# Retention: a head's output transposes behind all four gate projections, all convolution taps and the norm's root on VectorE

## The chip, the cores and the metric

The program runs on one NeuronCore of a Trainium2 chip. The metric is the device time of one execution in microseconds (us), lower is better. Engines are named as in the profile: PE (TensorE's matmuls), PEld (its weight loads), DVE (VectorE), ACT (ScalarE), POOL (GpSimd), SP (the engine whose queue starts the weight transfers).

## What is computed

Two transformer-like blocks over 512 tokens of width 1024, in float32. The change lies in the second block's mixer, in the stage that computes bidirectional retention (four heads, value width 512 per head) and, beside it, a convolution branch. Cut to these:

```python
q, k, v, rg, cv, ga, gb = split(u @ w_in)
q, k = rope_2d(heads(q, 256)), rope_2d(heads(k, 256)) * scale
o = bidir_retention(q, k, v, log_gf, log_gb, rf, rb)      # per head: decayed scores @ v, 512 x 512

# retention_branch: normalise each token of each head, gate it
mu, var = mean(o, -1), mean(square(o - mu), -1)
of = (o - mu) * rsqrt(var + 1e-6) * gn_w
y_ret = (silu(rg) * of) @ w_ret_out

# conv_branch: 31 taps along the tokens, each channel by itself
a, g = split(cv)
y = depthwise_conv(a * sigmoid(g), conv_w, width=31) + conv_b
y = silu(layernorm(y)) @ w_conv_out
mixed = (sigmoid(ga) * y_ret + sigmoid(gb) * y_conv) @ w_out
```

## The kernel before

Activations lie transposed: 128 channels on the partitions, 512 tokens in the free dimension. Each float32 operand is split in two parts of lower precision, hi (a cast on ACT) and lo (the difference, on DVE or POOL; `split`, line 110 and 111), and each product is three matmuls (`mm3`, lines 144 to 146). A projection of 128 output channels is eight chunks of 1024 input channels, so 24 matmuls into one of three PSUM buffers named `mm`. Its weight comes through a SP transfer, ACT's `whi` and a `wlo`, into one of three pairs of buffers: the weight of the projection three places on can be split only when the present one has ended.

`retention` runs over four heads. For each: `qkv` (four rotary projections `rope` for q and k, then eight value tiles), `scores` (six tiles), two `conv_in` (the convolution's input, two projections each), `av` (the head's output `on`, four query blocks by 18 matmuls), and `finish` (four gate projections and the transposes of `on`). In `av`, ACT copies each block from PSUM, DVE takes mean and variance (`bn_stats`, `bn_aggr`), and the reciprocal root of the four variances is found by three Newton steps on 128x4 tiles; then four DVE instructions (line 1264) normalise `on` in place.

`finish` transposes `on` on PE, four 128x128 transposes for each of the head's four channel groups c (tile `gt`, two PSUM buffers), and DVE multiplies each by weight and gate (`gtd`, line 1278) before POOL's queue writes it to DRAM (`gt_d`).

The convolution's taps are spread over these stages. A tap is one DVE instruction (line 1148, `cz` += weight times a shifted `cy`); taps are queued by `conv_in` and issued by `conv_step` in portions (`TAPS_QK`, `TAPS_V`, `TAPS_IN`, `TAPS_GATE` after a rotary projection, a value tile, a `conv_in`, a gate). Of the 31 taps of each of eight channel groups, 25 run on DVE; six (`CONV_POOL`) are multiplied by ACT (`cpr`) and summed by POOL (`z2`, line 1164), and DVE adds that sum (line 1152). POOL's queue then writes `cz` to DRAM.

The order on each engine is not that of the code alone: a list scheduler with its own time model places instructions; `issue_after` bounds the place of a transpose from below. Behind the last head `mix_out` starts with nine gate projections whose `wlo` are made on POOL (`wpool = (1,)`), then reads the convolution back.

Of the kernel before, what the change touches and what calls it, by code (L numbers as in the profile page):

```python
# [9 lines left out]
F32 = mybir.dt.float32  # L10
F32R = mybir.dt.float32r
I32 = mybir.dt.int32
AF = mybir.ActivationFunctionType
ALU = mybir.AluOpType
# [27 lines left out]

PV_ORDER = ((0, 0), (0, 1), (0, 3), (0, 2), (1, 0), (1, 1), (1, 3), (1, 2))

TAPS_QK, TAPS_V, TAPS_IN, TAPS_GATE = 4, 2, 5, 4
CONV_POOL = 6

GATES_FIRST = 9

# [14 lines left out]
class Kern:  # L64
# [1057 lines left out]
    def retention(self, U):  # L1122
        nc, a, s, tc, tmp = self.nc, self.a, self.small, self.tc, self.tmp
        with ExitStack() as st:
# [1 line left out]
            vp = st.enter_context(tc.tile_pool(reuse_waits=RW, name="convp", bufs=4))  # L1126
            rtab = rp.tile([128, 144], F32, name="rtab")
            nc.gpsimd.dma_start(out=rtab, in_=a["rtab"])
            taps, ptaps = [], []
            cw0 = VEC["cw"][0]  # L1130

            def conv_in(c):
                pa = self.proj(a["w_cv"][c], U)
                pg = self.proj(a["w_cv"][8 + c], U)
                sg = tmp.tile([128, 512], F32, tag="g", name="sg")
                nc.scalar.activation(out=sg, in_=pg, func=AF.Sigmoid)
                y = vp.tile([128, 544], F32, tag="cy", name="cy")
                nc.vector.memset(y[:, 0:15], 0.0)
                nc.vector.memset(y[:, 527:544], 0.0)
                nc.vector.tensor_tensor(out=y[:, 15:527], in0=sg, in1=pa, op=ALU.mult)  # L1140
                z = tmp.tile([128, 512], F32, tag=("lnk", "accd", "accq")[c % 3], name="cz", bufs=1)

                def tap(t):
                    w = self.vec[:, cw0 + c * 31 + t:cw0 + c * 31 + t + 1]
                    if t == 0:
                        nc.vector.tensor_scalar(out=z, in0=y[:, 0:512], scalar1=w, scalar2=self.v("cb", c), op0=ALU.mult, op1=ALU.add)
                    else:
                        nc.vector.scalar_tensor_tensor(out=z, in0=y[:, t:t + 512], scalar=w, in1=z, op0=ALU.mult, op1=ALU.add)  # L1148
                    if t == 30 - CONV_POOL:
                        while ptaps and ptaps[0][0] is ptap:  # L1150
                            ptap(ptaps.pop(0)[1])
                        nc.vector.tensor_tensor(out=z, in0=z, in1=z2, op=ALU.add)
                        nc.gpsimd.dma_start(out=self.z_d[c], in_=z)

                taps.extend((tap, t) for t in range(31 - CONV_POOL))
                prev = None
                z2 = vp.tile([128, 512], F32, tag="z2", name="z2", bufs=2)

                def ptap(t):
                    nonlocal prev  # L1160
                    p = vp.tile([128, 512], F32, tag="cpr", name="cpr", bufs=3)
                    nc.scalar.activation(out=p, in_=y[:, t:t + 512], func=AF.Copy, scale=self.vec[:, cw0 + c * 31 + t:cw0 + c * 31 + t + 1])
                    if prev is not None:
                        nc.gpsimd.tensor_tensor(out=z2, in0=prev, in1=p, op=ALU.add)
                        prev = z2
                    else:
                        prev = p

                ptaps.extend((ptap, t) for t in range(31 - CONV_POOL, 31))

            def conv_step(n):
                for q, m in ((ptaps, max(1, n // 3)), (taps, n)):
                    for _ in range(min(m, len(q))):
                        f, t = q.pop(0)
                        f(t)

            def rope(c, col, tag):
                ps = self.proj(a["w_qk"][c], U)
# [15 lines left out]
            def qkv(hd):  # L1194
                r = {}
                for tag, o in (("q", 0), ("k", 8)):
                    r[tag] = []
                    for col in range(2):
                        r[tag].append(rope(o + 2 * hd + col, col, tag))
                        conv_step(TAPS_QK)  # L1200
                r["td"] = rp.tile([128, 1536], F32, tag="td", name="td")
                nc.gpsimd.dma_start(out=r["td"], in_=self.td_d[hd])
                kc = self.wraw.tile([128, 1024], F32, tag="raw", name="kcr")[:, 0:512]
                nc.gpsimd.dma_start(out=kc, in_=self.kc_d[hd])
                r["kc"] = tuple(rp.tile([128, 512], F32R, tag=f"kc{i}", name=f"kc{i}") for i in "hl")
                self.split(kc, *r["kc"])
                r["v"] = [tuple(rp.tile([128, 512], F32R, tag=f"v{i}{tb}", name=f"v{i}{tb}") for i in "hl") for tb in range(4)]
                for half in range(2):
                    ws = [self.wload(a["w_v"][hd, half, i]) for i in range(2)]
                    for tb in range(4):  # L1210
                        ps = self.ps_mm.tile([128, 512], F32, tag="mm", name="mm")[:, 0:256]
                        self.vproj(ps, ws, U, tb)
                        cs = slice(half * 256, half * 256 + 256)
                        self.split(ps, r["v"][tb][0][:, cs], r["v"][tb][1][:, cs])
                        conv_step(TAPS_V)
                vc = self.wraw.tile([128, 1024], F32, tag="raw", name="vcr")
                nc.gpsimd.dma_start(out=vc, in_=self.vc_d[hd])
                vt = tuple(rp.tile([128, 1024], F32R, tag=f"vc{i}", name=f"vc{i}") for i in "hl")
                self.split(vc, *vt)
                r["vc"] = [tuple(t[:, 512 * i:512 * i + 512] for t in vt) for i in range(2)]  # L1220
                return r
# [22 lines left out]
            def av(hd, r, sc):  # L1244
                os = []
                mv = s.tile([128, 8], F32, tag="gmv", name="gmv")
                for qb in range(4):
                    qs = slice(qb * 128, qb * 128 + 128)
                    ps = self.ps_mm.tile([128, 512], F32, tag="mm", name="mm")
                    vs = r["v"] + r["vc"]  # L1250
                    for b in range(6):
                        self.mm3(ps, tuple(t[:, qs] for t in sc[b]), vs[b], b == 0, b == 5)
                    t = rp.tile([128, 512], F32, tag=("kh0", "kl0", "kh1", "kl1")[qb], name="on")
                    nc.scalar.copy(t, ps)
                    bs = s.tile([128, 6], F32, tag="bns", name="bns")
                    nc.vector.bn_stats(out=bs, in_=t)
                    nc.vector.bn_aggr(out=mv[:, 2 * qb:2 * qb + 2], in_=bs)
                    os.append(t)
                var = s.tile([128, 4], F32, tag="var", name="gvar")
                mv2 = mv.rearrange("p (q t) -> p q t", t=2)  # L1260
                nc.vector.tensor_scalar(out=var, in0=mv2[:, :, 1], scalar1=1e-6, scalar2=None, op0=ALU.add)
                rs = self.rsqrt(var, 4, e=nc.gpsimd)
                for qb in range(4):
                    nc.vector.tensor_scalar(out=os[qb], in0=os[qb], scalar1=mv[:, 2 * qb:2 * qb + 1], scalar2=rs[:, qb:qb + 1],
                                            op0=ALU.subtract, op1=ALU.mult)
                return os

            def finish(hd, os):
                gates, ends = [], []

                def out(c):
                    ch = 4 * hd + c
                    pt = self.ps_t.tile([128, 512], F32, tag="t", name="gt")
                    with tc.issue_after(ends[-1].ins):
                        for qb in range(4):
                            nc.tensor.transpose(out=pt[:, qb * 128:qb * 128 + 128], in_=os[qb][:, c * 128:c * 128 + 128], identity=self.ident)
                    t = tmp.tile([128, 512], F32, tag="t", name="gtd")
                    nc.vector.scalar_tensor_tensor(out=t, in0=pt, scalar=self.v("gnw", ch), in1=gates[c], op0=ALU.mult, op1=ALU.mult)
                    nc.gpsimd.dma_start(out=self.gt_d[ch // 2][:, (ch % 2) * 512:(ch % 2) * 512 + 512], in_=t)

                for c in range(4):
                    ps = self.proj(a["w_rg"][4 * hd + c], U)
                    ends.append(self.last_mm)
                    sg = tmp.tile([128, 512], F32, tag="g", name="sg")
                    nc.scalar.activation(out=sg, in_=ps, func=AF.Silu)
                    gates.append(sg)
                    if c > 0:
                        out(c - 1)
                    conv_step(TAPS_GATE)
                out(3)  # L1290

            for hd in range(4):
                r = qkv(hd)
# [226 lines left out]
```

## Time and profile before

| | |
|---|---|
| median of 3 runs | 3168.19 us (3163.14 to 3169.09) |
| the profiled execution | 3168.4 us, span of the profile 3166.6 us |
| mean granted TensorE clock | 0.982 of full speed |
| busy: PE, DVE, ACT, POOL | 96%, 60%, 38%, 14% of the span |
| retention's four heads | from about 2000 us to 2510 us of the span |

The profile shows one execution. A busy share over the whole span says little about a stage; what an engine waited for, and who released it, is listed for each wait. PE's instructions overlap (a matmul's duration is about 390 ns where a new one starts each 227 ns), so time on PE is read from start to start. The granted clock is that of PE: 1.00 is 2.4 GHz, 0.50 is 1.2 GHz.

### The profile page before, as it was taken

The numbers are of one execution on the slowest core, as the hardware profiler recorded it, in microseconds if no ns is written. First come the engines' busy times: TensorE is split into PE (matmuls) and PEld (weight loads), VectorE is DVE, ScalarE is ACT, GpSimd is POOL, SyncE is SP. The second block draws the span as 40 slices with busy tenths as digits, with TensorE's granted clock in tenths as the row PEclk, the third lists the DMA queues.
The fourth block names the chain that finished last, engine by engine and source line by source line (L and its number), as shares of the span: only waits on it lengthen the run. The fifth ranks groups of instructions, "written<-read, shape, count | busy, mean of one in ns | idle before, by whom it ended". The sixth has DMA issues, their size and how long they took to land.

```text
span 3166.6 us, 41034 instructions
## 1 busy us (share of the span) xinstructions
PE 3046.1 (96%) x15961; PEld 2578.1 (81%) x15961; DVE 1888.0 (60%) x3425; ACT 1192.0 (38%) x1956; POOL 455.0 (14%) x457
## 2 busy tenths in 40 slices
PE   8999999999999999999999999989889899999998
PEld 6678888887778888898888888878778787888887
DVE  4888657575888554473323347687786645553334
ACT  4774322244765222262121127334233243342222
POOL 2320000043310000130000001031121543200000
PEclk9999999999999999999999999999999999999999
DMA  4232445322323554322212126522323324333322
GB/s 131 73 96 75 153 146 186 125 83 79 91 84 101 160 172 130 97 94 85 74 52 76 54 81 220 168 79 95 97 70 104 106 80 146 107 100 94 100 92 62
DMA packets 103650, 334.08 MB, mean 106 GB/s; under 512 B 13164, under 2 KB 16364, under 8 KB 103328
## 3 DMA queue, kind: packets, MB, share of 16 engines
q1 hardware_dynamic: 89232, 289.83, 29.1%
q0 software_dynamic: 13136, 40.59, 4.1%
q8 instruction: 125, 2.05, 0.3%
q10 hardware_dynamic: 1088, 1.05, 0.1%
q14 instruction: 69, 0.57, 0.1%
HBM read 312.51 MB, written 14.71 MB: 103 GB/s over the span
## 4 chain that ended last, share of the span: by engine, by line
PE 58%; DVE 9%; issue 3%; ACT 2%; POOL 1%; DMA 1%; POOLq 0%; DVEq 0%; ACTq 0%
PE mm L145 17%; PE mm L144 17%; PE mm L146 17%; DVE cz L1148 4%; PE gc L144 1%; PE gc L146 1%; PE gc L145 1%; DVE wlo L111 1%; PE dc L146 1%; PE dc L145 1%; PE dc L144 1%; ACT whi L110 0%; PE rs L144 0%; PE rs L145 0%; PE rs L146 0%
## 5 line engine op out<-in xcount | busy, mean ns | idle before, releaser
L110 ACT CAST whi<-raw 128x1024 fp32r<-128x1024 f32 (+3 forms) x524 | 506.6, 968 | 1422.6 <-PE mm L145 1187.0
L145 PE MATMUL mm<-ul,whi 128*128 128x512 f32 (+2 forms) x2288 | 867.0, 380 | 2.1 <-POOL ul L271 1.6
L144 PE MATMUL mm<-uh,whi 128*128 128x512 f32 (+2 forms) x2288 | 866.7, 381 | 0.7 <-ACT cl L645 0.3
L146 PE MATMUL mm<-uh,wlo 128*128 128x512 f32 (+2 forms) x2288 | 864.7, 379 | 1.0 <-DVE wlo L111 0.6
L111 DVE TENSOR_TENSOR wlo<-raw,whi 128x1024 fp32r<-128x1024 f32 (+3 forms) x437 | 505.5, 1158 | 362.9 <-ACT whi L110 355.6
L145 PEld LDWEIGHTS mm<-ul,whi 128*128 128x128 f32 (+1 forms) x2288 | 433.2, 189 | 82.8 <-POOL ul L271 3.2
L146 PEld LDWEIGHTS mm<-uh,wlo 128*128 128x128 f32 (+1 forms) x2288 | 432.5, 189 | 83.2 <-POOL wlo L111 0.9
L144 PEld LDWEIGHTS mm<-uh,whi 128*128 128x128 f32 (+1 forms) x2288 | 432.3, 190 | 81.2 <-ACT uh L267 1.0
L144 PE MATMUL mm<-hh,whi 128*128 128x512 f32 (+1 forms) x789 | 293.6, 372 | 1.4 <-DVE acc L986 0.7
L145 PE MATMUL mm<-hl,whi 128*128 128x512 f32 (+1 forms) x789 | 293.0, 371 | 0.0
L146 PE MATMUL mm<-hh,wlo 128*128 128x512 f32 (+1 forms) x789 | 292.1, 371 | 0.3 <-DVE wlo L111 0.3
L528 DVE TENSOR_TENSOR g<-g,mm 128x512 f32<-128x512 f32 (+1 forms) x96 | 61.7, 643 | 276.9 <-PE mm L146 273.5
L111 POOL TENSOR_TENSOR wlo<-raw,whi 128x1024 fp32r<-128x1024 f32 (+2 forms) x87 | 184.0, 2117 | 236.0 <-ACT whi L110 231.4
L1148 DVE SCALAR_TENSOR_TENSOR cz<-cy,vec,cz 128x512 f32<-128x512 f32 x192 | 176.8, 942 | 2.5
L144 PEld LDWEIGHTS mm<-hh,whi 128*128 128x128 f32 x789 | 151.1, 191 | 27.0 <-issue 1.1
L146 PEld LDWEIGHTS mm<-hh,wlo 128*128 128x128 f32 x789 | 150.7, 191 | 26.6 <-DVE wlo L111 0.7
L145 PEld LDWEIGHTS mm<-hl,whi 128*128 128x128 f32 x789 | 150.9, 191 | 24.8 <-issue 0.2
L986 DVE SCALAR_TENSOR_TENSOR acc<-mm,g,acc 128x512 f32<-128x512 f32 (+1 forms) x61 | 43.1, 707 | 146.8 <-PE mm L146 146.8
L203 POOL TENSOR_TENSOR accd<-acc,acc 128x512 f32<-128x512 f32 x2 | 6.5, 3240 | 650.2 <-DVE acc L483 650.2
L146 PE MATMUL gc<-uch,wlo 128*128 128x256 f32 x352 | 99.4, 282 | 0.2 <-DVE wlo L111 0.2
L144 PE MATMUL gc<-uch,whi 128*128 128x256 f32 x352 | 99.1, 282 | 0.0
L145 PE MATMUL gc<-ucl,whi 128*128 128x256 f32 x352 | 99.0, 281 | 0.0
(407 smaller groups left out, 5230.7 us busy)
## 6 DMA issues: line engine op xcount, KB each, us to landing
mr<-w_mod SPq DMA_DIRECT2D x72, 512.0 KB, 3.9
raw<-w_f1i SPq DMA_DIRECT2D x54, 512.0 KB, 3.5
raw<-w_gate SPq DMA_DIRECT2D x44, 512.0 KB, 3.6
raw<-w_up SPq DMA_DIRECT2D x44, 512.0 KB, 3.5
raw<-w_f2i SPq DMA_DIRECT2D x44, 512.0 KB, 3.5
raw<-w_in SPq DMA_DIRECT2D x36, 512.0 KB, 3.8
raw<-w_v SPq DMA_DIRECT2D x32, 512.0 KB, 4.1
raw<-w_qk SPq DMA_DIRECT2D x24, 512.0 KB, 3.8
```

Of the source, the lines that this page charges most:

```text
L110: nc.scalar.copy(hi, src)
L111: (nc.gpsimd if pool else nc.vector).tensor_tensor(out=lo, in0=src, in1=hi.bitcast(F32), op=ALU.subtract)
L144: mm(out=ps, lhsT=w[0], rhs=x[0], start=first, stop=False)
L145: mm(out=ps, lhsT=w[0], rhs=x[1], start=False, stop=False)
L146: self.last_mm = mm(out=ps, lhsT=w[1], rhs=x[0], start=False, stop=last)
L203: e.tensor_tensor(out=st["accd"][:, sl], in0=(st["D0"] if m == 1 else st["accd"])[:, sl], in1=D[:, sl], op=ALU.add)
L528: gm = nc.vector.tensor_tensor(out=g, in0=g, in1=pu, op=ALU.mult)
L986: self.nc.vector.scalar_tensor_tensor(out=h, in0=ps, scalar=g[:, m:m + 1], in1=h, op0=ALU.mult, op1=ALU.add)
L1148: nc.vector.scalar_tensor_tensor(out=z, in0=y[:, t:t + 512], scalar=w, in1=z, op0=ALU.mult, op1=ALU.add)
```

## The change

Four things, all within `retention`. The transposes of a head's output are no longer placed after the second, third and fourth gate projection: all four gate projections come first, then two groups of transposes, and the other two after the next head's first two rotary projections (for the last head, all four at once). For this the four gates stay in the buffers `sh0` to `sh3` of the scores. All 31 taps of a channel group are DVE instructions; the multiplications on ACT and the sums on POOL are gone, and `TAPS_GATE` is 5. The Newton steps of the norm's root run on DVE rather than POOL.

```diff
-TAPS_QK, TAPS_V, TAPS_IN, TAPS_GATE = 4, 2, 5, 4
-CONV_POOL = 6
+TAPS_QK, TAPS_V, TAPS_IN, TAPS_GATE = 4, 2, 5, 5
...
-                    if t == 30 - CONV_POOL:
-                        while ptaps and ptaps[0][0] is ptap:
-                            ptap(ptaps.pop(0)[1])
-                        nc.vector.tensor_tensor(out=z, in0=z, in1=z2, op=ALU.add)
+                    if t == 30:
                         nc.gpsimd.dma_start(out=self.z_d[c], in_=z)
 
-                taps.extend((tap, t) for t in range(31 - CONV_POOL))
-                prev = None
-                z2 = vp.tile([128, 512], F32, tag="z2", name="z2", bufs=2)
-
-                def ptap(t):
-                    nonlocal prev
-                    p = vp.tile([128, 512], F32, tag="cpr", name="cpr", bufs=3)
-                    nc.scalar.activation(out=p, in_=y[:, t:t + 512], func=AF.Copy, scale=self.vec[:, cw0 + c * 31 + t:cw0 + c * 31 + t + 1])
-                    if prev is not None:
-                        nc.gpsimd.tensor_tensor(out=z2, in0=prev, in1=p, op=ALU.add)
-                        prev = z2
-                    else:
-                        prev = p
-
-                ptaps.extend((ptap, t) for t in range(31 - CONV_POOL, 31))
+                taps.extend((tap, t) for t in range(31))
 
             def conv_step(n):
-                for q, m in ((ptaps, max(1, n // 3)), (taps, n)):
-                    for _ in range(min(m, len(q))):
-                        f, t = q.pop(0)
-                        f(t)
+                for _ in range(min(n, len(taps))):
+                    f, t = taps.pop(0)
+                    f(t)
...
                         r[tag].append(rope(o + 2 * hd + col, col, tag))
+                        flush(1)
                         conv_step(TAPS_QK)
...
-                rs = self.rsqrt(var, 4, e=nc.gpsimd)
+                rs = self.rsqrt(var, 4)
...
+            late = []
+
             def finish(hd, os):
                 gates, ends = [], []
 
-                def out(c):
+                def out(c, after):
...
-                    with tc.issue_after(ends[-1].ins):
+                    with tc.issue_after(after.ins):
...
                 for c in range(4):
                     ps = self.proj(a["w_rg"][4 * hd + c], U)
-                    ends.append(self.last_mm)
-                    sg = tmp.tile([128, 512], F32, tag="g", name="sg")
+
+                    sg = rp.tile([128, 512], F32, tag=f"sh{c}", name="sg")
                     nc.scalar.activation(out=sg, in_=ps, func=AF.Silu)
                     gates.append(sg)
-                    if c > 0:
-                        out(c - 1)
                     conv_step(TAPS_GATE)
-                out(3)
+
+                late.extend(lambda after, c=c: out(c, after) for c in range(4))
+                flush(2 if hd < 3 else 4)
+
+            def flush(n):
+                for _ in range(min(n, len(late))):
+                    late.pop(0)(self.last_mm)
```

What the scheduler makes of it, at three places.

On DVE in the second head, from the last variance to the normalised output (`gvar` is the variance, `rsi` to `rsy` the root, `on` the output, `cz` a tap), before:

```order
L1257 BN_AGGR gmv<-bns 128x2
L1148 SCALAR_TENSOR_TENSOR cz<-cy,vec,cz 128x512
L1261 TENSOR_SCALAR gvar<-gmv 128x4
L1148 SCALAR_TENSOR_TENSOR cz<-cy,vec,cz 128x512
L158 TENSOR_SCALAR rsi<-gvar 128x4
L1148 SCALAR_TENSOR_TENSOR cz<-cy,vec,cz 128x512
L160 TENSOR_SCALAR rsj<-rsi 128x4
L1148 SCALAR_TENSOR_TENSOR cz<-cy,vec,cz 128x512 x3
L1264 TENSOR_SCALAR on<-on,gmv,rsy 128x512 x4
```

and the last rows of the same place in the changed kernel:

```order
L1147 SCALAR_TENSOR_TENSOR cz<-cy,vec,cz 128x512
L169 SCALAR_TENSOR_TENSOR rsy<-rst,rsy 128x4
L1147 SCALAR_TENSOR_TENSOR cz<-cy,vec,cz 128x512
L165 TENSOR_TENSOR rst<-rsy 128x4
L1147 SCALAR_TENSOR_TENSOR cz<-cy,vec,cz 128x512
L166 TENSOR_TENSOR rst<-rst,rsx 128x4
L1147 SCALAR_TENSOR_TENSOR cz<-cy,vec,cz 128x512
L169 SCALAR_TENSOR_TENSOR rsy<-rst,rsy 128x4
L1147 SCALAR_TENSOR_TENSOR cz<-cy,vec,cz 128x512
L1246 TENSOR_SCALAR on<-on,gmv,rsy 128x512 x4
L1147 SCALAR_TENSOR_TENSOR cz<-cy,vec,cz 128x512
```

Before, only the root's first two rows stand here, the rest on POOL, and no row of taps is between the third of three taps and `on`; now all of the root stands here, nearly each of its rows followed by one tap (11 taps and one `wlo` stand between `gvar` and `on`, and two more taps ahead of `gvar`).

On PE behind the last head (`gt` are the transposes, the rows after them the first of `mix_out`'s gate projections), before:

```order
L146 MATMUL mm<-uh_17097,wlo 128x512
L1276 MATMUL gt<-ident,on 128x128 x8
L144 MATMUL mm<-uh_17083,whi 128x512
L145 MATMUL mm<-ul_17084,whi 128x512
L146 MATMUL mm<-uh_17083,wlo 128x512
```

and in the changed kernel:

```order
L145 MATMUL mm<-uh_17097,wlo 128x512
L1260 MATMUL gt<-ident,on 128x128 x8
L143 MATMUL mm<-uh_17083,whi 128x512
L144 MATMUL mm<-ul_17084,whi 128x512
L145 MATMUL mm<-uh_17083,wlo 128x512
L1260 MATMUL gt<-ident,on 128x128 x4
L143 MATMUL mm<-uh_17085,whi 128x512
L1260 MATMUL gt<-ident,on 128x128 x4
L144 MATMUL mm<-ul_17086,whi 128x512
L145 MATMUL mm<-uh_17085,wlo 128x512
```

Before, two groups of four stand one and two projections earlier, and eight transposes come last; now all sixteen stand here, the third and fourth group three and four matmuls behind the first two.

On DVE at the same place in the changed kernel:

```order
L166 TENSOR_TENSOR rst<-rst,rsx 128x4
L1147 SCALAR_TENSOR_TENSOR cz<-cy,vec,cz 128x512
L169 SCALAR_TENSOR_TENSOR rsy<-rst,rsy 128x4
L1147 SCALAR_TENSOR_TENSOR cz<-cy,vec,cz 128x512
L1246 TENSOR_SCALAR on<-on,gmv,rsy 128x512 x4
L1147 SCALAR_TENSOR_TENSOR cz<-cy,vec,cz 128x512 x12
L1262 SCALAR_TENSOR_TENSOR gtd<-gt,vec,sg 128x512 x2
L1147 SCALAR_TENSOR_TENSOR cz<-cy,vec,cz 128x512 x4
L1262 SCALAR_TENSOR_TENSOR gtd<-gt,vec,sg 128x512 x2
L1147 SCALAR_TENSOR_TENSOR cz<-cy,vec,cz 128x512 x4
L190 TENSOR_TENSOR z_22348<-z_22348,lnk 128x512
```

There are twelve taps between the normalised output and the first `gtd`, which frees the PSUM buffer of the third group of transposes. On POOL at the same place (`wlo` are the splits of `mix_out`'s weights), before:

```order
L173 TENSOR_TENSOR rsy<-rst,rsy 128x4
L1153 DMA z_d<-cz 128x512
L111 TENSOR_TENSOR wlo<-raw,whi 128x1024
L1279 DMA gt_d<-gtd 128x512
L111 TENSOR_TENSOR wlo<-raw,whi 128x1024
L1279 DMA gt_d<-gtd 128x512
L1153 DMA z_d<-cz 128x512
L111 TENSOR_TENSOR wlo<-raw,whi 128x1024
```

and in the changed kernel:

```order
L1149 DMA z_d<-cz 128x512
L110 TENSOR_TENSOR wlo<-raw,whi 128x1024 x2
L1149 DMA z_d<-cz 128x512
L110 TENSOR_TENSOR wlo<-raw,whi 128x1024
L1263 DMA gt_d<-gtd 128x512 x4
L1310 DMA z_22348<-z_d 128x512
L1310 DMA z_22357<-z_d 128x512
L110 TENSOR_TENSOR wlo<-raw,whi 128x1024
```

Before, a split came after each write of `gtd`; now three splits stand ahead of the first `gt_d`.

## Rows read from the trace of the kernel before

**Rows 1.** The page, busy time by engine: microseconds, share, instructions.

```profile
PE 3046.1 (96%) x15961; PEld 2578.1 (81%) x15961; DVE 1888.0 (60%) x3425; ACT 1192.0 (38%) x1956; POOL 455.0 (14%) x457
```

**Rows 2.** Waits of TensorE in 2060 to 2516: in total, times, longest.

```profile
PE gt L1276 <- DVE on L1264: 33.2, 4, 8.3
PE gt L1276 <- DVE gtd L1278: 1.4, 1, 1.4
```

**Rows 3.** Busy time, granted clock, DMA share and rate over one head's period.

```profile
2090.87:2217.54 126.67, 118.37 (x606) 100.51 (x605) 98.86 (x136) 43.08 (x60) 26.05 (x33) 0.96 0.28 92
```

**Rows 4.** TensorE in time order around head 0's transposes: start, us, instruction, idle before.

```profile
2101.53 0.39 PE L146 MATMUL mm<-uh,wlo 128*128 128x512 f32 x1
2110.22 1.84 PE L1276 MATMUL gt<-ident,on 128*128 128x128 f32 x4 [8.30 <-DVE on L1264]
2111.72 0.77 PE L144 MATMUL mm<-uh,whi 128*128 128x512 f32 x1
2112.29 0.63 PE L145 MATMUL mm<-ul,whi 128*128 128x512 f32 x1
...
2116.12 0.40 PE L145 MATMUL mm<-ul,whi 128*128 128x512 f32 x1
...
2119.32 0.60 PE L1276 MATMUL gt<-ident,on 128*128 128x128 f32 x4
2119.68 0.47 PE L144 MATMUL mm<-uh,whi 128*128 128x512 f32 x1
2119.99 0.39 PE L145 MATMUL mm<-ul,whi 128*128 128x512 f32 x1
```

**Rows 5.** Busy time and granted clock within and after that gap.

```profile
2101.90:2110.20 8.30, 0.02 (x1) 0.00 (x0) 5.59 (x14) 1.38 (x2) 4.34 (x13) 0.74 0.00 0
2110.30:2115.20 4.90, 4.90 (x12) 3.38 (x13) 4.87 (x10) 0.00 (x0) 0.62 (x1) 0.50 0.26 81
```

**Rows 6.** GpSimd in time order: first and last of the root's 13 instructions.

```profile
2103.56 0.68 POOL L162 TENSOR_SCALAR rsx<-gvar 128x4 f32<-128x4 f32 x1 [11.31 <-DVE gvar L1261]
...
2109.38 0.20 POOL L173 TENSOR_TENSOR rsy<-rst,rsy 128x4 f32<-128x4 f32 x1
```

**Rows 7.** VectorE in time order through the same root.

```profile
2101.32 0.69 DVE L1256 BATCH_NORM_STATS2 bns<-on 128x6 f32<-128x512 f32 x1
...
2103.30 0.17 DVE L1261 TENSOR_SCALAR gvar<-gmv 128x4 f32<-128x4 f32 x1
2103.37 0.75 DVE L1148 SCALAR_TENSOR_TENSOR cz<-cy,vec,cz 128x512 f32<-128x512 f32 x1
...
2109.62 1.92 DVE L1264 TENSOR_SCALAR on<-on,gmv,rsy 128x512 f32<-128x512 f32 x4 [2.71 <-POOL rsy L173]
```

**Rows 8.** VectorE instructions grouped by line, 2066 to 2512.

```profile
L1148 DVE SCALAR_TENSOR_TENSOR cz<-cy,vec,cz 128x512 f32<-128x512 f32 x192 | 176.8, 942 | 2.5
```

**Rows 9.** The chain that ended last, behind the last head: start, us, what.

```profile
2498.80 0.76 DVE cz L1148
...
2499.59 2.99 DVE cz L1148
...
2502.61 0.76 DVE cz L1148
```

**Rows 10.** GpSimd in time order, same stretch.

```profile
2499.63 2.39 POOL L111 TENSOR_TENSOR wlo<-raw,whi 128x1024 fp32r<-128x1024 f32 x1 [0.68 <-ACT whi L110]
```

**Rows 11.** TensorE in time order, same stretch.

```profile
2506.44 0.66 PE L1276 MATMUL gt<-ident,on 128*128 128x128 f32 x4 [1.41 <-DVE gtd L1278]
```

**Rows 12.** VectorE in time order, head 1's first rotary projection.

```profile
2132.27 0.69 DVE L1184 TENSOR_TENSOR rp<-mm,rtab 128x512 f32<-128x512 f32 x1 [0.66 <-DMA gt_d<-gtd]
...
2136.91 0.69 DVE L111 TENSOR_TENSOR ql<-rp,qh 128x512 fp32r<-128x512 f32 x1 [0.69 <-ACT qh L110]
2137.52 0.69 DVE L1184 TENSOR_TENSOR rp<-mm,rtab 128x512 f32<-128x512 f32 x1
```

**Rows 13.** VectorE in time order, behind the last head.

```profile
2558.01 2.02 DVE L191 TENSOR_TENSOR z<-z,lnk 128x512 f32<-128x512 f32 x1 [46.56 <-ACT lnk L190]
```

More of the change, by code (lines that the diff above doesn't have):

```diff
@@ L1128, in retention @@
             nc.gpsimd.dma_start(out=rtab, in_=a["rtab"])
-            taps, ptaps = [], []
+            taps = []
             cw0 = VEC["cw"][0]
```

## The prediction

> **What bounds the kernel now.** I read the page first: PE is busy for 96% of the span and no other engine for more than 60% (its weight loads aside) [rows 1], so time can only come out of PE's waits and out of the clock that it is granted. Then PE's waits in retention: there is one kind that matters, the transposes `gt` waiting for the normalised output `on`, four times (once per head) 8.3 us, and one wait of 1.4 for `gtd` [rows 2]. Apart from these PE runs without a gap through the stage; that is the reason to look at nothing but this place, and at what could become a new wait.
>
> PE in time order shows the whole price of one gap [rows 4]. The last matmul of the second gate starts at 2101.53, so the next would start 0.227 later, at 2101.76. The transposes start at 2110.22: 8.46 lost. They are then slow: 1.50 us to the next matmul and 0.57 to the one after, where the following group of four takes 0.36 and 0.31: 1.40 lost. Nine matmuls then take 3.83 us (2112.29 to 2116.12) instead of 9 x 0.227 = 2.04: 1.79 lost. The granted clock says why: 0.74 over the gap and 0.50, the lower of the two levels, behind it [rows 5]. So a gap costs 8.46 + 1.40 + 1.79 = 11.65. The other three heads show the same pattern (8.46 to 8.50 lost, the same 1.4, and 1.5 to 1.6 on the slow matmuls): 11.5, 11.4 and 11.4. The last head adds its 1.4 wait [rows 11]. In all 11.65 + 11.5 + 11.4 + 12.8 = 47.4 us.
>
> What the gap waits for: DVE's last `bn_stats` starts at 2101.32, POOL's root runs from 2103.56 to 2109.58 [rows 6], and the four normalising instructions end at 2111.5 [rows 7]; DVE idles 2.7 ahead of them. The `bn_stats` is itself late, 10.45 us behind the head's last output matmul (about 2090.87, where the period of [rows 3] begins).
>
> **The change part by part.**
>
> *All taps on DVE.* 48 multiplications leave ACT, 40 sums leave POOL, eight additions leave DVE, and 48 taps come. The 192 taps of before take 176.8 us, 0.94 each [rows 8]; one that meets no POOL work is 0.75 long and the next starts 0.66 later, on another tile [rows 7], or 0.78 later on the same one [rows 9]. 192 x 0.72 would be 138, so 38 us, 9.5 a head, go to something that I take to be the POOL sums running beside them, since a tap beside a POOL split shows the same thing more strongly: 2.99 instead of 0.76 [rows 9, 10]. With the sums gone this returns, and the 48 new taps cost 48 x 0.72 = 35. DVE's load is even: about 99 us in a head's period of 126.7 [rows 3], about 99 in the 115 that will be left (86%). It hides beside PE's projections. It also brings the last `bn_stats` forward by those 9.5 us, to about 1.5 us behind the head's last matmul, counting a copy and a little backlog (bounds 0.9 and the 10.45 of before).
>
> *The root on DVE.* Between that `bn_stats` and the end of `on` the order has 13 taps, a weight split, some 16 small instructions and four normalising ones: 0.6 + 13 x 0.66 + 1.14 + 16 x 0.08 (a small one to the next instruction, 2103.30 to 2103.37 [rows 7]) + 1.9 = 13.5. So `on` is ready 15 us behind the head's last matmul; with all its bounds at their worst, 24.
>
> *Transposes behind four gates.* PE reaches them after four projections, 4 x 24 x 0.227 = 21.8 us. That is 6.8 later than `on`: the gap goes, with its clock loss, in heads 0 to 2 entirely, 34.5 us. At the worst bound 2 us of wait remain in each. The number of transposes is the same.
>
> *What is queued behind them now.* The two deferred groups come after the next head's first and second rotary projection. Their `gtd` and the taps enter DVE's tightest stretch: a rotary projection takes DVE 5.25 us [rows 12], of which 0.7 are idle before `ql`, against PE's 24 x 0.227 = 5.44. Now it has 0.66 + 0.66 to 0.78 more, less the idle: about 5.85 and so 0.4 of lag for each of four, after a start about 1.7 late; some 2 to 3 us of lag at the value tiles. Three PSUM buffers cover two projections, 10.9 us there, then two value tiles, 5.8. I take 0. If the cover failed it would be up to 4 us a head, 12 in all.
>
> The tiles of `gtd` and of the rotary projection share two buffers, so a projection must wait for a `gt_d` transfer to land. It did before (0.66 idle [rows 12]), and by the order the first `gt_d` now starts some 5 us ahead of the need; 0. The POOL queue issues `z_d`, the head's next `kcr` and then `gt_d`: all three are ready by 20 us behind the head's last matmul; 0.
>
> *The last head.* Here `on` is followed by twelve taps and only then by `gtd`, which frees the PSUM buffer for the third group of transposes. PE wants that group at 21.8 + 0.9 (eight transposes) + 0.7 (three matmuls) = 23.3 behind the last matmul. DVE: five taps that alternate at 0.66 and seven on one tile at 0.78 make 8.8, from 15.0 to 23.8, and `gtd` 0.7: 24.5 even alone. But POOL now splits `mix_out`'s weights there. The weight of the projection three on can be split when a gate ends, so POOL starts about 1.1 behind the second, third and fourth gate, at 12, 17.5 and 22.9, for 2.39 each [rows 10], all ahead of the first `gt_d` in its queue. Each holds up one DVE instruction by 2.99 - 0.76 = 2.2 [rows 9]; the first meets the chain or `on`. With two of them `gtd` ends at 28.9, with three at 31.1: PE waits 5.6 to 7.8, say 6.5. That is between the gap of 8.3, which lost the clock, and that of 1.4, behind which four transposes take 0.66 and not 1.84 [rows 4, 11]; nearer to the first, so I add 2.9 (1.40 and some 1.5 on slow matmuls, as above). The last head then pays 9.4 instead of 12.8 and saves 3.4.
>
> Later, DVE stands idle for 46.6 us behind the last head [rows 13], which hides the eight more taps left there.
>
> **Sum.** 34.5 + 3.4 = 38 us. 3168.4 (the profiled execution, which is the median within 0.2) - 38 = 3130.
>
> The Trainium skill (Perfetto Trace Analysis, Optimizing Scalar/DVE Operations) says that where DVE is saturated, moving some work to ScalarE or even GpSimd may make sense; by it this change goes the wrong way. It adds that the two share a read port, so that the move may not help. The trace agrees with the second part (a tap of 2.99 beside a POOL split). With the first part the result would be the rival D below.
>
> **Rivals.**
>
> *B, no wait in the last head*: the collisions fall elsewhere, or taps run faster. Then all 47.4 are saved: 3121. For it: the timing of three splits within 11 us decides. Against it: DVE is 1.2 late there without any.
>
> *C, DVE's lag reaches PE in the rotary and value stretch*: 4 us in three heads, 3142. For it: 5.25 of 5.44 is tight [rows 12]. Against it: two buffers of cover.
>
> *E, the wait is only moved*: `on` comes later than 21.8 in all heads, and the transposes stand as long as before: 3168. It needs 15 us more in a chain of 13.5; the 2.7 idle ahead of `on` [rows 7] shows that it was POOL and not DVE that was slow.
>
> *D, DVE becomes the bound, slower than before*: this needs DVE work of over 126.7 us in a head's period [rows 3], where I count 99. If POOL were not what slows the taps, 60 taps at 0.94 instead of 0.72 would add 13: 112, still under PE's 115. Above 126.7 each us costs four; at a tenth more, 4 x 12.7 = 51: 3219. Nothing in the rows carries it so far.
>
> **How the numbers follow.** A measurement of this kernel tells about 0.2% (6 us) from no change. Chances: my forecast 0.62, B 0.17, C 0.16, E 0.03, D 0.02. The likeliest gives 3130, by its own bounds 3126 to 3134. The range reaches to B less 4 of scatter, and to C: 3117 to 3143; it leaves out E, D and a tail of each side. Faster is the sum of forecast, B and C: 0.95; same 0.03; slower 0.02.
>
> **What would show it.** In the new profile: no wait of `gt` for `on` in heads 0 to 2, a granted clock of 1.00 through them, a period of 115 us; a wait of `gt` for `gtd` of 5 to 8 us behind the last head, with a clock of 0.5 after it; taps of 0.75 in the heads and of about 3 beside the three POOL splits; no wait of `mm` for a PSUM buffer in the rotary stretch. The prediction is wrong if `on` ends later than 21.8 us behind a head's last matmul, if PE waits at the value tiles, or if the last head's wait is absent or beyond 8.

## The result and the profile after

The changed kernel takes 3128.89 us (median of 4 runs, 3127.28 to 3131.53) where the kernel before takes 3168.64: a ratio of 0.9879, 95% interval 0.9862 to 0.9896. The forecast was 3130, its range 3117 to 3143. The profiled execution took 3128.61 us, its span is 3126.5.

The page, busy time by engine, as in [rows 1]:

```profile
PE 3034.5 (97%) x15961; PEld 2572.4 (82%) x15961; DVE 1877.0 (60%) x3505; ACT 1159.4 (37%) x1908; POOL 368.5 (12%) x365
```

POOL lost 86.5 us and ACT 33. DVE took over the work of both and is busy for less time than before, 1877 against 1888 us. VectorE's taps grouped by line, as in [rows 8], show why:

```profile
L1147 DVE SCALAR_TENSOR_TENSOR cz<-cy,vec,cz 128x512 f32<-128x512 f32 x240 | 178.0, 760 | 2.2
```

240 taps cost what 192 cost before (176.8): 48 taps came for nothing, because each is now 0.76 us instead of 0.94.

Waits of TensorE in 2060 to 2516, as in [rows 2]:

```profile
PE gt L1260 <- DVE gtd L1262: 6.5, 1, 6.5
```

The four waits of 8.3 us for the normalised output are gone. A single wait is left, 6.5 us, for `gtd`. The windows show three periods of a head, as in [rows 3], then the wait behind the last head, the 3 us after it and the next 4.6 (columns: PE, PEld, DVE, ACT, POOL, granted clock, DMA share, GB/s):

```profile
2090.64:2205.44 114.80, 114.80 (x605) 98.89 (x604) 95.74 (x156) 35.13 (x48) 4.87 (x9) 1.00 0.32 101
2205.44:2320.37 114.93, 114.93 (x605) 98.89 (x605) 95.79 (x156) 35.02 (x48) 4.86 (x9) 1.00 0.32 101
2320.37:2435.20 114.83, 114.83 (x605) 98.87 (x604) 95.67 (x152) 35.13 (x48) 4.32 (x8) 1.00 0.29 94
2458.60:2465.20 6.60, 0.17 (x1) 0.00 (x0) 6.42 (x8) 0.00 (x0) 2.26 (x1) 0.73 0.36 119
2465.30:2468.30 3.00, 3.00 (x11) 2.65 (x12) 2.89 (x5) 0.00 (x0) 1.09 (x2) 0.50 0.46 175
2468.40:2473.00 4.60, 4.60 (x22) 3.77 (x21) 4.49 (x7) 0.47 (x1) 2.14 (x4) 1.00 0.35 118
```

In the heads PE is busy without a break at a clock of 1.00. The kernel before has 126.67 in the first period [rows 3] and these in the next two:

```profile
2217.54:2343.99 126.45, 118.15 (x606) 100.39 (x605) 98.89 (x136) 43.12 (x60) 25.96 (x33) 0.96 0.30 92
2343.99:2470.38 126.39, 118.05 (x606) 100.34 (x605) 98.81 (x132) 43.02 (x60) 25.53 (x32) 0.96 0.27 86
```

A period is 11.5 to 11.8 us shorter than before. Three periods make 34.9 of the 40.1 us between the two spans.

VectorE in time order in the first head, as in [rows 7]; the head's output products end at 2090.64, where PE starts the gates:

```profile
2091.79 0.69 DVE L1238 BATCH_NORM_STATS2 bns<-on 128x6 f32<-128x512 f32 x1
...
2103.14 1.91 DVE L1246 TENSOR_SCALAR on<-on,gmv,rsy 128x512 f32<-128x512 f32 x4
```

and TensorE where it comes to the transposes, as in [rows 4]:

```profile
2112.18 0.39 PE L145 MATMUL mm<-uh,wlo 128*128 128x512 f32 x1
2112.41 1.04 PE L1260 MATMUL gt<-ident,on 128*128 128x128 f32 x8
2113.21 0.48 PE L143 MATMUL mm<-uh,whi 128*128 128x512 f32 x1
```

The last `bn_stats` starts 1.15 us behind the products (10.45 before) and `on` is ready at 2105.05, 14.4 behind. PE reaches the transposes at 21.8, and they start at once.

Behind the last head, whose products end at 2435.27, VectorE:

```profile
2447.78 3.98 DVE L1246 TENSOR_SCALAR on<-on,gmv,rsy 128x512 f32<-128x512 f32 x4
2451.68 12.88 DVE L1147 SCALAR_TENSOR_TENSOR cz<-cy,vec,cz 128x512 f32<-128x512 f32 x12
2464.48 1.40 DVE L1262 SCALAR_TENSOR_TENSOR gtd<-gt,vec,sg 128x512 f32<-128x512 f32 x2
```

GpSimd beside it:

```profile
2447.27 2.84 POOL L110 TENSOR_TENSOR wlo<-raw,whi 128x1024 fp32r<-128x1024 f32 x1 [71.94 <-ACT whi L109]
2452.70 2.63 POOL L110 TENSOR_TENSOR wlo<-raw,whi 128x1024 fp32r<-128x1024 f32 x1 [2.60 <-ACT whi L109]
...
2458.14 2.72 POOL L110 TENSOR_TENSOR wlo<-raw,whi 128x1024 fp32r<-128x1024 f32 x1
```

and TensorE:

```profile
2458.38 0.40 PE L145 MATMUL mm<-uh,wlo 128*128 128x512 f32 x1
2465.28 1.11 PE L1260 MATMUL gt<-ident,on 128*128 128x128 f32 x4 [6.51 <-DVE gtd L1262]
```

The three splits stand at 12.0, 17.4 and 22.9 behind the products. The first falls on the four normalising instructions, which take 3.98 instead of 1.91; the other two fall in the twelve taps, which take 12.88 where twelve of 0.74 would take 8.9. So `gtd` is late, and the third group of transposes with it.

### The profile page after: what moved, and what is told of

Same layout as the page of the kernel before. It is cut to its first block, busy times and chain, and to the rows that moved or that the text cites. A ratio compares the mean times of both kernels' runs of the same rounds, so it can differ in the third digit from the quotient of the medians.

```text
span 3126.5 us, 40929 instructions
## 1 busy us (share of the span) xinstructions
PE 3034.5 (97%) x15961; PEld 2572.4 (82%) x15961; DVE 1877.0 (60%) x3505; ACT 1159.4 (37%) x1908; POOL 368.5 (12%) x365
## 4 chain that ended last, share of the span: by engine, by line
PE 62%; DVE 5%; issue 2%; ACT 1%; POOL 1%; DMA 0%; POOLq 0%; DVEq 0%; ACTq 0%
PE mm L143 18%; PE mm L144 18%; PE mm L145 18%; DVE cz L1147 1%; PE gc L143 1%; PE gc L145 1%; PE gc L144 1%; PE dc L145 1%; PE dc L144 1%; PE dc L143 1%; DVE wlo L110 1%; PE rs L143 0%; PE rs L144 0%; PE rs L145 0%; ACT whi L109 0%
## 5 line engine op out<-in xcount | busy, mean ns | idle before, releaser
L330 ACT ACTIVATE P<-P,nm 128x128 f32<-128x128 f32 (+3 forms) x160 | 88.1, 552 | 18.2 <-DVE nm L326 17.6
```

Of the source, the lines that this page charges most:

```text
L330: nc.scalar.activation(out=sl, in_=sl, func=AF.Exp, scale=scale, bias=nm[:, qb:qb + 1], accum_out=sm[:, qb:qb + 1])
```

## The experiments

Two theories were open. The first, which the prediction leaned on: the new place of the transposes takes the gap away. The second: DVE, freed from POOL's sums beside it, delivers the output so early that the place does not matter. The medians (the ratio is to the kernel before on the same chip; its medians there were 3170.31, 3167.81 and 3167.69 for the three groups):

| run | us | ratio and 95% interval |
|---|---|---|
| after_again | 3130.21 | 0.9879, 0.9866 to 0.9893 |
| order_only | 3163.24 | 0.9986, 0.9977 to 0.9995 |
| old_order | 3128.98 | 0.9873, 0.9859 to 0.9887 |
| psum_last | 3121.19 | 0.9851, 0.9836 to 0.9865 |
| taps_only | 3128.08 | 0.9872, 0.9857 to 0.9887 |
| root_only | 3171.61 | 1.0010, 1.0001 to 1.0019 |
| dve_splits | 3120.63 | 0.9851, 0.9837 to 0.9864 |
| warm | 3182.48 | 1.0044, 1.0031 to 1.0056 |
| sums_back | 3163.70 | 0.9988, 0.9979 to 0.9997 |
| sums_old | 3172.17 | 1.0013, 1.0004 to 1.0023 |
| order_root | 3156.97 | 0.9967, 0.9955 to 0.9980 |

**after_again**: the changed kernel once more, beside the others.

> The changed kernel once more, on the same chip as the three beside it, as the mark for comparisons of a few us. Both theories: 3128 to 3130, 0.988 of the kernel before.

It repeated the result.

**order_only**: the kernel before with the new place alone (and the gates in `sh0` to `sh3`, as it needs).

```diff
                         r[tag].append(rope(o + 2 * hd + col, col, tag))
+                        flush(1)
...
-                    if c > 0:
-                        out(c - 1)
                     conv_step(TAPS_GATE)
-                out(3)
+                late.extend(lambda after, c=c: out(c, after) for c in range(4))
+                flush(2 if hd < 3 else 4)
...
```

> The kernel before with the new place of the transposes alone; six taps of each group stay on ACT and POOL, the root on POOL. Theory 1 (the place of the transposes carries the gain): the output is ready about 20.7 us behind a head's last matmul, as before, PE comes for it at 21.8, so heads 0 to 2 have no wait of more than 1 us and save 34. Behind the last head fourteen taps and a weight split now stand ahead of the first gtd, which is ready at about 36 to 38: a wait of some 13 with a lost clock, 3 more than before. About 3138. Theory 2 (the gain comes from relieving DVE of what POOL does to it): the output comes later than PE in every head, waits of 5 to 8 us stay, 3155 to 3168.

It gains 0.14%. The waits of TensorE in 2060 to 2516 say where the rest stays:

```profile
PE mm L146 <- DVE wlo L111: 19.7, 4, 4.9
PE gt L1279 <- DVE gtd L1281: 12.5, 4, 9.6
```

No wait for `on` is left, and yet 32 us of waits are. VectorE in time order, first head:

```profile
2115.89 1.92 DVE L1265 TENSOR_SCALAR on<-on,gmv,rsy 128x512 f32<-128x512 f32 x4 [2.70 <-POOL rsy L173]
2117.72 1.22 DVE L111 TENSOR_TENSOR wlo<-raw,whi 128x1024 fp32r<-128x1024 f32 x1
```

TensorE:

```profile
2118.99 0.71 PE L146 MATMUL mm<-uh,wlo 128*128 128x512 f32 x1 [4.91 <-DVE wlo L111]
```

`on` is ready 20.7 us behind the products (they end at 2097.13), before PE would come to the transposes. But the split of a gate's weight is queued behind `on` on DVE, and a gate now stands where the transposes stood. What waits for the late output is another instruction.

**old_order**: the changed kernel with the transposes back among the gates (the diff above, reversed).

> The changed kernel with the transposes back among the gates; all taps and the root on DVE. Theory 1: the output is ready 14.4 us behind the last matmul, PE comes for it after two gates, at 10.9 to 11.5, and waits 3 to 4 us in each head; whether the granted clock falls in such a gap is open (up to 3 us more a head). 3136 to 3150. Theory 2: DVE's relief is the gain, so most of the 40 us stay, 3128 to 3133.

It is as fast as the whole change, so the first theory falls. The waits of TensorE in 2060 to 2516:

```profile
PE gt L1257 <- DVE on L1245: 3.0, 4, 2.3
```

In three heads the wait is 0.23, in the last 2.3. With taps and root on DVE the scheduler itself puts the first transposes into the third gate. The products end at 2093.19, and the first transpose starts 13.1 us behind them, where the first block of `on` is just ready (PE wanted it at 10.9 in the kernel before):

```profile
2106.29 0.33 PE L1257 MATMUL gt<-ident,on 128*128 128x128 f32 x1 [0.23 <-DVE on L1245]
```

So the transposes are back among the gates here, but not at the very place of before.

**taps_only** and **root_only** divide the second theory; both keep the transposes among the gates. taps_only is the changed kernel with the old place and

```diff
-                rs = self.rsqrt(var, 4)
+                rs = self.rsqrt(var, 4, e=nc.gpsimd)
```

> All 31 taps on DVE; the root stays on POOL and the transposes stay where they were before, among the gates. Theory (it is the sums on POOL that slow the taps and delay the last bn_stats; this alone carries the gain): the last bn_stats starts within 2 us of the head's last output matmul, the root takes the 6.3 us that it took before, and the normalised output is ready some 11.5 us behind, where the transposes are wanted at 10.9: waits under 1.5 us a head, about 3130. Rival (the slow root on POOL is what the transposes wait for): a wait of some 8 us remains in each head, 3160 or more.

root_only is the kernel before with the opposite line.

> Only the root on DVE; the taps on ACT and POOL and the transposes among the gates, as before. Theory (the late bn_stats is the cause): it still starts some 10.5 us behind the head's last output matmul, and the chain of root, taps and normalising behind it takes 13.5 on DVE, so the output is ready at 24, later than before (20.6); the transposes, now placed a little later within the third gate (wanted at about 12.5), wait 8 to 11 us: 3165 to 3180, no gain. Rival (the root carries the gain): waits under 3 us, 3135.

taps_only gives the whole gain, root_only none. In taps_only, VectorE in the first head:

```profile
2091.08 0.68 DVE L1237 BATCH_NORM_STATS2 bns<-on 128x6 f32<-128x512 f32 x1
...
2099.37 1.92 DVE L1245 TENSOR_SCALAR on<-on,gmv,rsy 128x512 f32<-128x512 f32 x4 [2.71 <-POOL rsy L172]
```

The products end at 2089.92, and `on` is ready 11.4 behind them: earlier than in the changed kernel (14.4), though DVE stands 2.7 us for POOL's root. The last head's wait for `gtd` is 0.4 there. That taps_only is still not at 3121 goes with a head's period of some 116 us (114.9 in the changed kernel, so some 3 us in three heads) and with 4.1 us of waits for POOL's `wlo` in 2000 to 2640; why the period is longer stays open. In root_only `on` is ready 23.9 behind the products, 3.2 later than before, with this wait of TensorE in 2060 to 2516:

```profile
PE gt L1276 <- DVE on L1264: 40.7, 4, 12.1
```

**sums_back** and **sums_old** put POOL's 40 sums and ACT's 48 multiplications back as work whose result is not used, into the changed kernel and into old_order. All else is as there, so DVE also keeps the 48 taps that it does not have in the kernel before.

```diff
+                    if t == 24:
+                        while ptaps and ptaps[0][0] is ptap:
+                            ptap(ptaps.pop(0)[1])
...
                 taps.extend((tap, t) for t in range(31))
...
+                ptaps.extend((ptap, t) for t in range(25, 31))
...
-                for _ in range(min(n, len(taps))):
-                    f, t = taps.pop(0)
-                    f(t)
+                for q, m in ((ptaps, max(1, n // 3)), (taps, n)):
+                    for _ in range(min(m, len(q))):
+                        f, t = q.pop(0)
+                        f(t)
```

> The changed kernel, in which the 48 multiplications on ACT and the 40 sums on POOL are made as well, as in the kernel before, and their result is not used. Theory (the sums running on POOL slow DVE's taps by about 9.5 us a head): the taps' mean rises from 0.76 to about 0.92, the last bn_stats falls back to some 10 us behind the head's last output matmul, the normalised output is ready at about 24 where the transposes are wanted at 21.8: waits of 2 to 4 us a head come back, 3137 to 3150. Rival (what slowed the taps was not the sums): taps stay at 0.76, 3129 to 3131.

> The same sums put back, their result unused, in the kernel with all taps and the root on DVE but with the transposes at their old place among the gates (old_order, 3129). Theory (with DVE slowed by the sums the place of the transposes matters, 21.8 against some 13 to 16 behind the head's last output matmul): the output is ready at about 24, the transposes wait 8 to 11 us a head and the clock falls behind each wait, 3165 to 3180. Rival (the old place is as good here too): within 4 us of sums_back.

Work whose result nothing uses takes some 34 of the 38 us gained back in sums_back, and all of them in sums_old. VectorE's taps in sums_back, grouped by line:

```profile
L1147 DVE SCALAR_TENSOR_TENSOR cz<-cy,vec,cz 128x512 f32<-128x512 f32 x240 | 212.1, 902 | 2.3
```

The same 240 taps take 34.1 us more, 0.85 for each of the 40 sums. VectorE in time order, around the ends of the last sums of a channel group:

```profile
2090.53 1.68 DVE L1147 SCALAR_TENSOR_TENSOR cz<-cy,vec,cz 128x512 f32<-128x512 f32 x1
2092.14 1.78 DVE L1147 SCALAR_TENSOR_TENSOR cz<-cy,vec,cz 128x512 f32<-128x512 f32 x1
2093.84 0.74 DVE L1147 SCALAR_TENSOR_TENSOR cz<-cy,vec,cz 128x512 f32<-128x512 f32 x1
...
2095.85 2.70 DVE L1147 SCALAR_TENSOR_TENSOR cz<-cy,vec,cz 128x512 f32<-128x512 f32 x4
...
2102.45 0.68 DVE L1256 BATCH_NORM_STATS2 bns<-on 128x6 f32<-128x512 f32 x1
```

GpSimd:

```profile
2090.05 1.62 POOL L1163 TENSOR_TENSOR z<-z,cpr 128x512 f32<-128x512 f32 x1
2091.74 1.63 POOL L1163 TENSOR_TENSOR z<-z,cpr 128x512 f32<-128x512 f32 x1
```

The two taps that begin while a sum runs take 1.68 and 1.78 us, and each ends 0.55 behind the end of that sum (2091.67 and 2093.37). Behind the last sum a tap takes 0.74 again. ACT's multiplications are back too, so they are a rival cause. A tap with two of them beside it and no sum, VectorE and then ACT:

```profile
2068.72 0.75 DVE L1147 SCALAR_TENSOR_TENSOR cz<-cy,vec,cz 128x512 f32<-128x512 f32 x1
2068.13 1.34 ACT L1161 ACTIVATE cpr<-cy,vec 128x512 f32<-128x512 f32 x2 [0.76 <-DVE cy L1139]
```

It is as short as a tap alone, and so are all eight taps of this trace that meet a multiplication but nothing on POOL; it is the sums. The last `bn_stats` starts 10.47 us behind the products (they end at 2091.98), where it stood in the kernel before. The time, though, missed the expected 3137 to 3150. `on` is ready at 23.7, as expected, but the waits of TensorE in 2060 to 2520 are not those of the transposes alone:

```profile
PE gt L1278 <- DVE gtd L1280: 19.2, 4, 12.2
PE mm L144 <- DVE wlo L110: 6.9, 3, 2.4
PE mm L145 <- DVE wlo L110: 6.2, 7, 2.8
```

A head costs 122.9 us (its last output product starts at 2091.76, the next head's at 2214.64) against 114.8: 8 instead of 2 to 4, since weight splits and `gtd` queued behind `on` are late as well. That sums_old is slower than sums_back shows what the new place is worth where the output is late: 0.25%, some 8 us here, where the move alone (order_only) gave 4.

**order_root**: the new place and the root on DVE, the taps on ACT and POOL (order_only and root_only together).

> The new place of the transposes and the root on DVE; the taps on ACT and POOL as before. Theory (the sums make the output late, the place covers most of it): the last bn_stats is some 10 us late as before, the chain behind it 13.5, the output is ready at about 24: waits of 2 to 4 us a head, 3140 to 3152. Rival (place and root together suffice, the taps need not be moved): 3128 to 3132.

It misses both ranges, on the side of the first: 3157. `on` is ready at 23.8, and TensorE waits 16.3 for `gtd`, 4.5 for `on` and 2.3 for `wlo`. Against order_only the root on DVE seems to bring 6 us; the intervals touch, so its size stays open. Against root_only the new place brings 0.43%, some 14 us, though the two ran on different chips. So with the sums on POOL the place is worth 4 to 14 us; with the output early (old_order against the changed kernel) it is worth nothing that these runs can tell.

**dve_splits** and **psum_last** take up the last head's wait from two sides. dve_splits makes `mix_out`'s first three splits on DVE:

```diff
                 for m in range(m0, m1):
+                    self.wpool = (0,) if m < 3 else (1,)
                     ps = self.proj(a["w_gab"][m], U)
```

> The changed kernel with the first three weight splits behind the last head made on DVE in place of POOL. Theory (POOL's splits, each holding up a DVE instruction by some 2.2 us, make the last head's wait): the six taps that then stand between the normalised output and the first gtd, with two splits of 1.2 us each, run undisturbed, gtd ends at about 23.5 behind the last output matmul, the third group of transposes waits under 2 us and PE's clock is not lowered: 3121 to 3123. Rival (the length of DVE's own queue makes the wait, whoever makes the splits): a wait of 5 us or more remains, 3128 to 3131.

psum_last gives the last head's third and fourth group of transposes PSUM buffers of their own (those of the scores, free by then):

```diff
-                    pt = self.ps_t.tile([128, 512], F32, tag="t", name="gt")
+                    last = hd == 3 and c > 1
+                    pt = (self.ps_s if last else self.ps_t).tile([128, 512], F32, tag="s" if last else "t", name="gt")
```

> The changed kernel; behind the last head the third and fourth group of transposes go into the two PSUM buffers of the scores, idle there, so that PE needs no gtd to go on. Theory 1 (the wait of 6.5 us is for the PSUM buffer that gtd frees): the wait and the slow clock behind it go, 6.7 + 1.8 less, 3120, 0.985 of before. Rival: DVE's late gtd holds up the start of the next stage in another place (a weight split on POOL, a projection's PSUM buffer), and the wait returns there: 3126 to 3129.

Both take the wait and its clock loss away and are faster than the changed kernel by 0.28%, some 9 us. In psum_last no wait for `gtd` is left; in dve_splits `on` takes 1.90 again, and of the wait this remains:

```profile
PE gt L1260 <- DVE gtd L1262: 0.3, 1, 0.3
```

So POOL's splits make DVE late, and the PSUM buffer passes it on to PE. (With three splits more on DVE the scheduler places ten taps, not twelve, ahead of the first `gtd`.)

**warm**: the kernel before with unused matmuls in the gap.

```diff
+WARM = 34
...
+                    if c == 0:
+                        dm = self.ps_s.tile([128, 512], F32, tag="s", name="dm")
+                        with tc.issue_after(ends[-1].ins):
+                            for i in range(WARM):
+                                nc.tensor.matmul(out=dm, lhsT=U[0][0][:, 0:128], rhs=U[0][0], start=True, stop=True)
```

> The kernel before with 34 additional matmuls of 128x512 per head, of which nothing is used, ahead of the first transposes, so that PE works through most of the 8.3 us gap. Theory (behind a gap some 3.2 us a head are lost to the lower granted clock that follows the idle time): the clock stays at 1.00, the transposes and the matmuls behind them run at full rate, four times about 3.1 us return: 3155 to 3158 by the median of before on this chip. Rival (the slow matmuls behind the gap have another cause, for instance late weights): no change, 3168 to 3170.

It is slower by 0.44%, against both theories. TensorE in the first head:

```profile
2100.65 7.87 PE L1278 MATMUL dm<-uh 128*128 128x512 f32 x34
2109.13 1.70 PE L1282 MATMUL gt<-ident,on 128*128 128x128 f32 x4 [0.61 <-DVE on L1265]
2110.58 0.47 PE L145 MATMUL mm<-uh,whi 128*128 128x512 f32 x1
2110.89 0.39 PE L146 MATMUL mm<-ul,whi 128*128 128x512 f32 x1
2111.12 0.40 PE L147 MATMUL mm<-uh,wlo 128*128 128x512 f32 x1
...
2126.10 0.66 PE L1282 MATMUL gt<-ident,on 128*128 128x128 f32 x4 [3.00 <-DVE gtd L1284]
...
2127.51 0.63 PE L145 MATMUL mm<-uh,whi 128*128 128x512 f32 x1
2127.94 0.63 PE L146 MATMUL mm<-ul,whi 128*128 128x512 f32 x1
```

Two things are seen. Behind the filled gap the matmuls start 0.23 apart, so their slowness was the clock; but the four transposes still take 1.45 us: they follow the four normalising instructions, which end one by one, the last at 2110.44. And what PE gains there it loses again behind the fourth gate, waiting for `gtd` (14.3 us in eight waits over the four heads, the longest 3.3), after which the clock falls all the same (matmuls 0.43 apart). In the kernel before, DVE was right behind PE: time given back to PE alone becomes a wait.

## Why the prediction was right, and where its reasons were not

**What a gap costs.** Right in sum: the three periods fell by 11.8, 11.5 and 11.5, forecast 11.65, 11.5 and 11.4. One part had the wrong name: of the 1.40 us of slow transposes some 1.1 are not the clock's, since the transposes take 1.45 at full clock too (warm), and only the matmul behind them and the 1.5 to 1.8 after it are. All parts go with the wait, so the sum stands.

**All taps on DVE.** Right, and the assumption in it is now shown: POOL's sums slow the taps. Their price was taken as 38 us and is 34.1 (sums_back); in the 38 are also the two taps of before that POOL's splits hold up, such as the 2.99 of [rows 9]. The last `bn_stats` at 1.15 (forecast 1.5) and the DVE load of 95.7 us in 114.8 (forecast 99 in 115) follow. Rival D has nothing left. The sums cost DVE 34 us where the 48 taps cost about 35 (at 0.72). The Trainium skill (Perfetto Trace Analysis, Optimizing Scalar/DVE Operations) allows offloading to GpSimd where DVE is saturated, and warns that the two share a read port: by the 34 us, the warning decides here. The Trainium skill (SBUF — State Buffer, SBUF: two separate sides) calls the shared port a lock that is held for a whole instruction, the other engine standing still. The trace agrees: in sums_back each of the 35 taps that begin while a sum runs ends 0.55 us behind it, and each of the 40 sums but one ends 1.14 to 1.16 behind the end of the VectorE instruction that runs at its own start. The two take turns, and of a sum recorded as 1.62 us some 0.47 are its own wait; so it costs the taps 0.85 and not 1.62. A split of 2.84 us costs the normalising instructions 2.1.

**The root on DVE.** `on` ready at 14.4, forecast 15. But the step is no gain by itself: it makes the chain longer (root_only, 23.9 against 20.7), and without it the result is the same (taps_only).

**Transposes behind four gates.** This is the step that failed, though its number came out. It said that the gap goes because PE reaches the transposes at 21.8, later than `on`. In the changed kernel it does so, but this place is not what the gain needs: the 34.5 us (measured 34.9) are saved whether they are moved or not (old_order). With the taps on DVE, `on` comes at 11.4 (taps_only) or 14.4, and the scheduler finds a place for it among the gates; the move alone saves some 4 us (order_only). In that part the number came out by luck. The step's bound fails too: with `on` at 24 it saw 2 us a head at most, and sums_back with `on` at 23.7 loses 8. It counted only the transposes behind `on`, not the `wlo` of the next gates. For the same reason rival E was priced wrongly: it takes not 15 us more in the chain but only the sums back, and the time is 3163.

**What is queued behind them.** Right: no wait in the rotary stretch, so rival C did not come.

**The last head.** Right in mechanism and in the wait: three splits, at the times forecast, 6.5 us. The lower clock afterwards cost about 1.5 us, not 2.9 (3.04 from 2465.28 to 2468.32, for two groups of transposes at 0.36, the matmuls behind them at 0.31 [rows 4] and one at 0.23, together 1.57): it lasted 3 us, and no normalising instruction stood in between. psum_last and dve_splits, at 3121, give the time of rival B, which says that this wait and its slow clock, within the scatter, were all that lay between the two.

## What to carry to other kernels

Work moved to GpSimd is not off VectorE where both run at once: compare the duration of VectorE's instructions beside it and away from it, and count the excess against what was moved. Before an instruction that PE waits for is given more time, list everything else queued behind its producer, the weight splits above all; the wait goes to the next of them. And where one version moves several things, run each alone: here the total was right and one of its causes was not.

## What the runs showed of the hardware

Behind a wait of PE of 3.00 us the granted clock fell (warm; 0.62 over the next 3.4 us), where one of 1.41 [rows 11] was not followed by slow matmuls; behind 6.5 us it stayed at 0.50 for 3.0 us, behind 8.3 for 4.9 at least [rows 5]. Behind a shorter wait, 2.27 us in the last head of old_order (PE goes on at 2454.43), it fell as well, to 0.53 here:

```profile
2455.40:2459.00 3.60, 3.60 (x11) 2.85 (x11) 2.98 (x5) 0.00 (x0) 0.55 (x1) 0.53 0.32 132
```

And an addition on POOL of 128x512, whose result nobody reads, adds 0.85 us to VectorE's taps: a tap that begins beside it ends 0.55 behind it (the two shown with sums_back take 1.68 and 1.78 in place of 0.74). A `bn_stats` beside a sum is not held up: in sums_back one takes 0.68 at 2088.74, within a sum from 2088.35 to 2089.97.
